# Half tiles of weights, whole float32 attention products, and a planner that counts issue time

## The chip, the core and the metric

The kernel runs on one core of a Trainium2 chip. The metric is device time in microseconds of one execution, the median of three. The engines of a core are TensorE (PE in the profile; its weight loads are PEld), VectorE (DVE), ScalarE (ACT), GpSimd (POOL) and SyncE (SP); each runs its own instruction stream in order, and DMA transfers are issued from SP, ACT and POOL. SBUF is the on-chip memory, PSUM the eight accumulator banks that TensorE writes.

## What is computed

One attention layer of a decoder and a final norm; `DEPTH` is 1, so the convolution layer does not run. There are 256 rows, a model width of 4096 and 32 heads of 128, all in float32.

```python
def attn_branch(xn, w_in, w_out):
    q, k, v, g = jnp.split(xn @ w_in, 4, axis=-1)     # 256x4096 @ 4096x16384
    o = stick_breaking_attention(heads(q), heads(k), heads(v))
    return (o * jax.nn.silu(g)) @ w_out               # 256x4096 @ 4096x4096

# per head, with z = q k^T / sqrt(128), for s < t:
log_fail = where(causal, log_sigmoid(-z), 0)
suffix   = cumsum(log_fail, reverse=True) - log_fail
a        = where(causal, exp(log_sigmoid(z) + suffix), 0)
out      = a @ v
# whole program
h   = x + attn_branch(rms_norm(x, norm_attn), w_in, w_out)
out = rms_norm(h, final_norm)
```

## The kernel before

**Split products.** A float32 operand is written as the sum of two float32r tiles, a high part (a cast on ACT) and a low part (full minus high, on DVE). One product is three TensorE passes: high by high, high by low, low by high (`mm3`, lines 752 to 758). The 335 MB of weights are split this way as they arrive: `piece` (lines 394 to 404) casts `raw` to `wh` on ACT and writes `wl` on DVE.

**Units and steps.** The projection by `w_in` is 16 units; unit u makes q and k, then gate and v, of two heads. The projection by `w_out` is a plain unit (number 16), two mixed units (17 and 18) and two single ones (19 and 20). A unit has 16 steps along the contraction, 256 rows of weights each. A mixed unit runs Strassen-like products: a step of the list `SEVEN` has seven products, the others eight, collected in seven PSUM banks `b1` to `b7`, which `combine` (lines 654 to 696) adds up on DVE and ACT into `qk_sb` and `gv_sb` (in the out projection, into the `h` tiles). A product is three matmuls of 128 by 128 by 512 columns, named `acc<-wh,nh`, `acc<-wl,nh` and `acc<-wh,nl` (`sh`, `oh`, `ph` and `rh` stand in place of `nh` in other units).

**Weights.** A step's weights are one quad: a `raw` tile of 8 KB in each partition, four slots of 512 columns, filled by four DMAs of 256 KB from SP (`load`, lines 341 to 360). A slot of 512 is two blocks of 256 columns, so the destination runs are 1 KB. There are three quads (`RAW_BUFS`), and a quad is given back when the low parts of all its pieces are written (`low_done`). For a seven step, `sums` (lines 375 to 392) adds slots in place, in three DVE instructions: one of 1024 columns and two of 512.

**Attention of a head** (`head`, lines 767 to 858): four transposes into `tr`; `tr` is split into `qkh` (ACT) and `qkl` (DVE); six matmuls give the scores `z`; ACT and DVE turn them into `f`, which is split into `fh` and `fl`; four matmuls scan; ACT makes `a`, which is split into `ah` (ACT) and `al` (DVE); v had been split once a unit into `vh` and `vl` (`v_parts`); six matmuls give `o`; DVE multiplies it by the gate.

**What sets the order.** All of it is decided ahead, while the program is built. `Plan` (lines 87 to 212) simulates the engines with fixed costs (`vector_ns`, `scalar_ns`, `tensor_ns`, and the issue costs in `moved`, line 320: 55 ns a DMA on SP, 900 on POOL). Each piece of work is a generator that waits for names (`until`), for rings of buffers (`take`, `give`) or for an engine (`work`). When an engine is free in the simulation, the waiting request with the smallest key, its due time, is written into that engine's stream. The chip then follows this order and waits wherever an input is late. Work for TensorE in `head` goes through `ten` (line 317), with a key ahead of all weight products, so it is put in as soon as the simulation has its inputs.

Every instruction is recorded through one helper, so the profile shows almost all of them under one line, L106; they are told apart by the names of their tiles.

Of the kernel before, what the change touches and what calls it, by code (L numbers as in the profile page):

```python
# [43 lines left out]
RAW_BUFS = 3  # L44
# [19 lines left out]
EIGHT_PARTS = (  # L64
    (slice(0, 2), ((2, "A11", 0), (2, "A12", 1), (4, "A21", 0), (4, "A22", 1))),
    (slice(2, 4), ((5, "A21", 0), (5, "A22", 1), (3, "S3", 0), (3, "S5", 1))),
# [3 lines left out]
def plain_part(place, one, two):  # L70

    return place, ((one, "A11", 0), (two, "A21", 0), (one, "A12", 1), (two, "A22", 1))
# [14 lines left out]
class Plan:  # L87
# [97 lines left out]
    def work(self, engine, cost, emit, key=None, after=None, hold=True, moves=()):  # L185

        def request(go):
            self.serial += 1  # L190
            item = (self.here if key is None else key, self.serial, cost, emit, after, go, hold, moves)
            heapq.heappush(self.waiting[engine], item)
            self.later(max(self.now, self.free[engine]), self.turn, engine)

        return request

    def turn(self, engine):
# [4 lines left out]
        end = self.now + cost  # L202
# [13 lines left out]
def kernel(  # L216
# [41 lines left out]
    for u, (kind, w, cols) in enumerate(units):  # L258
        for s in range(NS):
            if kind == "single":  # L260
# [3 lines left out]
                which = [plain_part(slice(2 * (s % 2), 2 * (s % 2) + 2), *b)]  # L264
            else:
                quads.append(tuple((w, c, s) for c in cols))
                if kind == "plain":
                    which = [
                        plain_part(slice(0, 2), PLAIN["C11"], PLAIN["C21"]),
                        plain_part(slice(2, 4), PLAIN["C12"], PLAIN["C22"]),  # L270
# [3 lines left out]
            for i, (place, prods) in enumerate(which):  # L274
                parts.append(
                    dict(u=u, s=s, i=i, last=i == len(which) - 1, place=place, prods=prods, quad=len(quads) - 1,
                         seven=which is SEVEN_PARTS, size=len(range(*place.indices(2 * KT))))
                )
# [30 lines left out]
    def dve(emit, n, key=None, **kw):  # L309
        cost = sum(vector_ns(m) for m in n) if isinstance(n, tuple) else vector_ns(n)  # L310
        return nc.work("vector", cost, emit, soon() if key is None else key, **kw)

    def act(emit, n, key=None, **kw):
        cost = sum(scalar_ns(m) for m in n) if isinstance(n, tuple) else scalar_ns(n)
# [15 lines left out]
    for name, places in (  # L330
        ("raw", RAW_BUFS), ("w", PAIRS), ("s", SINGLES), ("gh", 3), ("one", 1), ("two", 1), ("vh", 1), ("vl", 1),
        ("qkh", 1), ("qkl", 1), ("f", 1), ("ah", 1), ("al", 1), ("att", 1), ("heads", 1),
        *((f"b{b}", 1) for b in range(1, 8)),
    ):
        nc.ring(name, places)
# [3 lines left out]
    lows_left = {}  # L339

    def load():
        for q, given in enumerate(quads):
            yield nc.take("raw")
            raw[q] = wp.tile([P, 2 * KT, W], F32, tag="raw", name=f"raw{q}", bufs=RAW_BUFS)
            todo = []
            for k, (w, blocks, s) in enumerate(given):
                for chunks in ([slice(0, 1), slice(1, 2)] if q == 0 else [slice(0, 2)]):
                    to = slice(KT * k + chunks.start, KT * k + chunks.stop)
                    todo.append([
                        (raw[q][:, to, i * CW : (i + 1) * CW], w[c, s][:, chunks, :]) for i, c in enumerate(blocks)  # L350
                    ])
            for k, some in enumerate(todo):
                name = ("raw", q, k) if q == 0 else ("raw", q) if k else None
                yield moved(
                    "sync",
                    lambda some=some: [nc.sync.dma_start(*a) for a in some],
                    [W * (1 if q == 0 else KT) // 2] * 2,
                    quad_key[q],
                    after=name and (lambda name=name: nc.tell(name)),
                )  # L360

    quad_key, quad_parts = {}, {}
    for n, p in enumerate(parts):
        quad_key.setdefault(p["quad"], first[n])
        quad_parts.setdefault(p["quad"], []).append(n)

    def low_done(n):
        q = parts[n]["quad"]
        lows_left[n] -= 1
        if not lows_left[n]:  # L370
            nc.tell(("lows", n))
            if all(lows_left.get(m) == 0 for m in quad_parts[q]):
                nc.give("raw")

    def sums(q):

        a, b, c, d = quad_parts[q]
        r = raw[q]
        tt = nc.vector.tensor_tensor
        key = first[c] - 3.0 * 1e3  # L380
        yield nc.until(("lows", a), ("lows", b))
        yield dve(
            lambda: tt(
                out=r[:, 0:3:2, :], in0=r[:, 0:4:3, :], in1=r[:, 2:3, :].broadcast_to([P, 2, W]), op=ALU.add
            ),
            2 * W, key,
        )
        nc.tell(("sums", c))
        key = first[d] - 3.0 * 1e3
        yield dve(lambda: tt(out=r[:, 3, :], in0=r[:, 0, :], in1=r[:, 3, :], op=ALU.add), W, key)  # L390
        yield dve(lambda: tt(out=r[:, 1, :], in0=r[:, 3, :], in1=r[:, 1, :], op=ALU.add), W, key)
# [822 lines left out]
```

## Time and profile before

| | |
|---|---|
| median of 3 runs | 1800.3 us (1799.93 to 1800.44) |
| the profiled execution | 1805.19 us, span 1803.4 us |
| PE busy | 1768.4 us, 98% |
| DVE busy | 1611.2 us, 89% |
| ACT busy | 1145.4 us, 64% |
| weight DMAs on the SP queue | 1284, nearly all 256 KB, 4.6 to 4.8 us from issue to landing |
| bytes moved | 388 MB, 215 GB/s over the span |

The span is what the trace covers. The execution's own time is 1.8 us longer than its span, and 4.9 us over the median of the runs that were only timed. The end of a matmul is modelled in the trace, so a PE that starts a 512-column matmul every 0.23 us shows no idle time, though each is drawn 0.39 us long; the starts of matmuls tell its pace.

### The profile page before, as it was taken

To read this page: it belongs to the slowest core of one execution; us is meant where nothing else is said; L and a number is where in the kernel's file an instruction comes from. 1 tells how busy PE (TensorE), PEld (TensorE's weight loads), DVE (VectorE), ACT (ScalarE), POOL (GpSimd) and SP (SyncE) were. 2 spreads that over 40 slices of the span, in tenths; PEclk is the share of its full clock that TensorE was granted. 3 is DMA by queue.
4 is the path that set the end of the run, shared out by engine and by line. 5 is a ranking of instruction groups with operands and counts; after the bars stand their busy time and mean duration, and the time that the engine had idled before them with its cause. 6 is when DMAs were issued, how large, how long until landed. Compare 5 with 4: busy or idle time off the path is not lost.

```text
span 1803.4 us, 23678 instructions
## 1 busy us (share of the span) xinstructions
PE 1768.4 (98%) x8011; PEld 1450.0 (80%) x8011; DVE 1611.2 (89%) x1974; ACT 1145.4 (64%) x1568; POOL 67.0 (4%) x132
## 2 busy tenths in 40 slices
PE   9999999999999999999999999999999999999997
PEld 7888888878887888788888878887888778878786
DVE  6679999999999999999999999999999887999864
ACT  6675757576757675757575757675756565655543
POOL 0001000000000000000000000000002100000000
PEclk9999999999999999999999999999999999999999
DMA  9958575666666656575756565666669967678884
GB/s 319 318 179 269 153 221 181 211 195 206 182 212 193 214 181 212 180 233 171 231 175 223 177 214 190 202 197 194 202 189 279 310 190 226 215 226 254 252 270 159
DMA packets 373625, 388.01 MB, mean 215 GB/s; under 512 B 23808, under 2 KB 351744, under 8 KB 373504
## 3 DMA queue, kind: packets, MB, share of 16 engines
q1 hardware_dynamic: 357296, 352.15, 62.4%
q0 software_dynamic: 14624, 31.99, 5.6%
q10 hardware_dynamic: 1584, 2.38, 0.4%
q8 instruction: 62, 1.02, 0.2%
q14 instruction: 59, 0.48, 0.1%
HBM read 370.43 MB, written 15.99 MB: 214 GB/s over the span
## 4 chain that ended last, share of the span: by engine, by line
PE 63%; DVE 13%; DMA 10%; ACT 6%; issue 4%; SPq 3%; ACTq 0%; DVEq 0%
PE acc L106 59%; DMA raw<-in_w_in_dram 6%; DVE wl L106 6%; ACT wh L106 5%; DVE raw L106 4%; SPq L106 3%; DMA raw<-in_w_out_dram 3%; PE z L106 2%; PE o L106 1%; DVE gv_sb L106 1%; PE tr L106 1%; ACT f L106 0%; ACT qk_sb L106 0%; ACT h L106 0%; ACTq L106 0%
## 5 line engine op out<-in xcount | busy, mean ns | idle before, releaser
L106 ACT CAST wh<-raw 128x1024 fp32r<-128x1024 f32 (+1 forms) x898 | 857.5, 986 | 478.5 <-DVE raw L106 221.4
L106 DVE TENSOR_TENSOR wl<-raw,wh 128x1024 fp32r<-128x1024 f32 (+1 forms) x898 | 1003.1, 1142 | 138.5 <-ACT wh L106 124.0
L106 PE MATMUL acc<-wh,nh 128*128 128x512 f32 x1680 | 662.9, 395 | 0.0
L106 PE MATMUL acc<-wl,nh 128*128 128x512 f32 x1680 | 656.2, 391 | 1.0 <-DVE wl L106 0.6
L106 PE MATMUL acc<-wh,nl 128*128 128x512 f32 x1680 | 655.2, 390 | 0.0
L106 PEld LDWEIGHTS acc<-wl,nh 128*128 128x128 f32 x1680 | 315.9, 188 | 68.2 <-DVE wl L106 7.5
L106 PEld LDWEIGHTS acc<-wh,nl 128*128 128x128 f32 x1680 | 315.4, 188 | 66.5
L106 PEld LDWEIGHTS acc<-wh,nh 128*128 128x128 f32 x1680 | 315.7, 188 | 61.2
L106 DVE TENSOR_TENSOR raw<-raw 128x512 f32<-128x512 f32 (+1 forms) x384 | 332.6, 866 | 6.8
L106 PE MATMUL acc<-wl,ph 128*128 128x512 f32 x304 | 119.2, 392 | 3.5 <-DVE wl L106 3.3
L106 PE MATMUL acc<-wh,ph 128*128 128x512 f32 x304 | 118.8, 391 | 0.8 <-DVE h L106 0.8
L106 PE MATMUL acc<-wh,pl 128*128 128x512 f32 x304 | 118.4, 389 | 0.0
L106 PE MATMUL acc<-wh,sh 128*128 128x512 f32 x256 | 101.8, 398 | 0.6 <-DVE sh L106 0.6
L106 PE MATMUL acc<-wh,sl 128*128 128x512 f32 x256 | 101.1, 395 | 0.8 <-DVE sl L106 0.8
L106 PE MATMUL acc<-wl,sh 128*128 128x512 f32 x256 | 100.8, 394 | 0.0
L106 PEld LDWEIGHTS acc<-wl,ph 128*128 128x128 f32 x304 | 57.1, 188 | 17.9 <-DVE wl L106 6.3
L106 PEld LDWEIGHTS acc<-wh,ph 128*128 128x128 f32 x304 | 57.1, 188 | 14.6 <-DVE h L106 1.5
L106 PEld LDWEIGHTS acc<-wh,pl 128*128 128x128 f32 x304 | 57.1, 188 | 11.6
L106 PEld LDWEIGHTS acc<-wh,sl 128*128 128x128 f32 x256 | 48.7, 190 | 11.7 <-DVE sl L106 1.5
L106 PEld LDWEIGHTS acc<-wh,sh 128*128 128x128 f32 x256 | 48.9, 191 | 11.3 <-issue 1.5
L106 PEld LDWEIGHTS acc<-wl,sh 128*128 128x128 f32 x256 | 48.9, 191 | 9.9
L106 ACT CAST qkh<-tr 128x512 fp32r<-128x512 f32 x32 | 18.8, 588 | 56.6 <-PE tr L106 56.5
(130 smaller groups left out, 1393.8 us busy)
## 6 DMA issues: line engine op xcount, KB each, us to landing
raw<-in_w_in_dram SPq DMA_DIRECT2D x1020, 256.0 KB, 4.6
raw<-in_w_out_dram SPq DMA_DIRECT2D x256, 256.0 KB, 4.8
xr<-in_x_dram SPq DMA_DIRECT2D x16, 256.0 KB, 5.7
xn<-in_xT_dram POOLq DMA_DIRECT2D x16, 256.0 KB, 4.0
xres<-in_x_dram SPq DMA_DIRECT2D x16, 256.0 KB, 5.3
xs<-in_xT_dram SPq DMA_DIRECT2D x15, 256.0 KB, 5.7
spill_f<-gated POOLq DMA_DIRECT2D x15, 256.0 KB, 3.6
spill_h<-oh POOLq DMA_DIRECT2D x15, 256.0 KB, 5.1
```

What stands on the lines that cost most here:

```text
L106: return self.tc.keep_in_program_order(getattr(self.engine, name)(*args, **kw))
```

## The change

- **Half tiles.** A quad becomes two `raw` tiles of 4 KB in each partition, one for each pair of column blocks, laid out block by block, so that a DMA of 256 KB writes runs of 2 KB. There are seven such tiles in place of three quads. Each is given back by itself (`tile_done`). `sums` makes four DVE instructions of 512 columns in place of three. The third and fourth part of a seven step are grouped anew (banks 7 and 6, then 5 and 4).
- **Whole products.** The scores and attention times v take float32 operands, with one matmul where there were three: `tr` is only copied (`qkT`, ACT), `a` and v are used as they are. `v_parts`, `qkl`, `ah` and `al` are gone. The scan keeps its split.
- **The planner's numbers.** A DMA on SP or ACT costs 330 ns. An ACT instruction that starts after idle time costs 50 ns more; grouped instructions are costed one by one with 122 or 100 ns between them. A request by `ten` is only entered 400 ns after its inputs are there.
- **Room.** Two `h` tiles of column block 5 move to the ring `s`; the early `xs` tiles use `qkh` and `qkl` in place of `vh` and `vl`, and the constant `neg_tri` is made earlier, to free `qkl`.

```diff
-RAW_BUFS = 3
+RAW_BUFS = 7
+BOTH, SECOND = slice(0, 2), slice(1, 2)
 SEVEN_PARTS = (
-    (slice(0, 2), ((1, "A11", 0), (2, "A12", 1))),
-    (slice(3, 4), ((3, "S4", 0),)),
-    (slice(0, 3, 2), ((5, "S1", 0), (7, "S3", 1))),
-    (slice(1, 4, 2), ((4, "A22", 0), (6, "S2", 1))),
+    (0, BOTH, ((1, "A11", 0), (2, "A12", 1))),
+    (1, SECOND, ((3, "S4", 0),)),
+    (1, BOTH, ((7, "S3", 0), (6, "S2", 1))),
+    (0, BOTH, ((5, "S1", 0), (4, "A22", 1))),
 )
...
+            if wait:
+                self.later(self.now + wait, ready, go)
...
-        end = self.now + cost
+        end = self.now + cost + (50 if engine == "scalar" and self.now > self.free[engine] else 0)
...
+    FULL_P, FULL_S = (P,) * 4, (S,) * 4
     def ten(emit, *n):
-        return nc.work("tensor", sum(tensor_ns(m) for m in n), emit, nc.here - 1e4)
+        return nc.work("tensor", sum(tensor_ns(m) for m in n), emit, nc.here - 1e4, wait=400)
     def moved(engine, emit, sizes, key, after=None, hold=False, adds=False):
-        issue = {"sync": 55, "gpsimd": 900, "scalar": 90}[engine]
+        issue = 900 if engine == "gpsimd" else 330
...
+            for t, (w, blocks, s) in enumerate(given):
+                yield nc.take("raw")
+                r = raw[q, t] = wp.tile([P, HG, KT, CW], F32, tag="raw", name=f"raw{q}_{t}", bufs=RAW_BUFS)
...
+                    def both():
+                        for i, c in enumerate(blocks):
+                            nc.sync.dma_start(r[:, i, chunks, :], w[c, s][:, chunks, :])
...
+    def tile_done(*tile):
+        tile_left[tile] -= 1
+        if not tile_left[tile]:
+            nc.give("raw")
...
+        yield nc.until(("lows", a), ("raw", q, 1))
+        yield add(one, 0, one[:, :, 0, :], two[:, :, 0, :], first[c])
+        yield add(two, 0, two[:, :, 0, :], two[:, :, 1, :], first[c])
+        yield nc.until(("lows", b))
+        yield add(two, 1, two[:, :, 1, :], one[:, :, 0, :], first[c])
+        nc.tell(("sums", c))
+        yield add(one, 1, one[:, :, 1, :], two[:, :, 1, :], first[d])
...
-        yield act(lambda: nc.scalar.copy(qh, tr), 2 * S)
-        yield dve(lambda: minus(ql, tr, qh), 2 * S)
+        qk = ap.tile([P, 2, S], F32, tag="qkh", name=f"qkT{u}_{i}")
+        yield act(lambda: nc.scalar.copy(qk, tr), 2 * S)
...
-            mm3(z[:, 0:P], k(slice(P, S)), q(slice(P, S)), True, False)
-            mm3(z[:, P:BW], k(slice(0, P)), q(slice(0, S)), False, True)
+            nc.tensor.matmul(z[:, 0:P], qk[:, 1, P:S], qk[:, 0, P:S], start=True, **kw)
+            nc.tensor.matmul(z[:, P:BW], qk[:, 1, 0:P], qk[:, 0, :], start=False, **kw)
...
-        yield act(lambda: nc.scalar.copy(ah, a), BW)
-        yield dve(lambda: minus(al, a, ah), BW)
...
-            mm3(o, v(0), (ah[:, P:BW], al[:, P:BW]), True, False)
-            mm3(o[:, P:S], v(1), (ah[:, 0:P], al[:, 0:P]), False, True)
+            nc.tensor.matmul(o, v(0), a[:, P:BW], start=True, stop=False, **kw)
+            nc.tensor.matmul(o[:, P:S], v(1), a[:, 0:P], start=False, stop=True, **kw)
```

The order moves in two places that the prediction speaks of. The first is on TensorE, at the change from unit 8 to unit 9 (`acc8_3` is the last bank of unit 8; `tr8_0` the transposes of its first head; `z8_0` its scores). Before:

```order
L106 MATMUL acc8_3_6748<-wh399_7397,nh15_1987 128x512
L106 MATMUL acc8_3_6748<-wl399_7398,nh15_1987 128x512
L106 MATMUL acc8_3_6748<-wh399_7397,nl15_1988 128x512
L106 MATMUL tr8_0_7483<-ident_118,qk_sb8_7409 128x128 x4
L106 MATMUL acc8_3_6748<-wh399_7397,nh15_1987 128x512
L106 MATMUL acc8_3_6748<-wl399_7398,nh15_1987 128x512
L106 MATMUL acc8_3_6748<-wh399_7397,nl15_1988 128x512
L106 MATMUL acc9_2_7496<-wh400_7416,nh0_1047 128x512
```

With the change:

```order
L108 MATMUL acc8_3_6702<-wl399_7344,nh15_1961 128x512
L108 MATMUL acc8_3_6702<-wh399_7343,nl15_1962 128x512
L108 MATMUL acc9_2_7438<-wh400_7359,nh0_1067 128x512
L108 MATMUL acc9_2_7438<-wl400_7360,nh0_1067 128x512
L108 MATMUL acc9_2_7438<-wh400_7359,nl0_1068 128x512
L108 MATMUL tr8_0_7437<-ident_100,qk_sb8_7353 128x128 x4
L108 MATMUL acc9_2_7438<-wh400_7359,nh0_1067 128x512
L108 MATMUL acc9_2_7438<-wl400_7360,nh0_1067 128x512
```

The transposes stand six matmuls later: 16 in place of 10 after the last one into bank 4, whose sum they read. In both orders the scores follow soon, nine matmuls after the transposes before and six with the change; the third step of both heads' chains, the scan, stands 48 and 30 matmuls after the scores in both.

The second place is the SP queue in unit 18, where steps of the out projection load weights (`raw296` and on) between rows of x (`xres`). Before:

```order
L106 DMA xres3_0_14977<-in_x_dram 128x512
L106 DMA raw296_14986<-in_w_out_dram 128x2x256 x4
L106 DMA raw297_15001<-in_w_out_dram 128x2x256 x4
L106 DMA xres3_1_15068<-in_x_dram 128x512
L106 DMA raw298_15076<-in_w_out_dram 128x2x256 x4
L106 DMA raw299_15093<-in_w_out_dram 128x2x256 x4
```

With the change:

```order
L108 DMA xres3_0_14894<-in_x_dram 128x512
L108 DMA raw297_0_14897<-in_w_out_dram 128x512 x2
L108 DMA raw297_1_14911<-in_w_out_dram 128x512 x2
L108 DMA raw298_0_14918<-in_w_out_dram 128x512 x2
L108 DMA raw298_1_14977<-in_w_out_dram 128x512 x2
L108 DMA xres3_1_14985<-in_x_dram 128x512
L108 DMA raw299_0_14992<-in_w_out_dram 128x512 x2
```

Each quad's four DMAs become two pairs, each pair behind a wait of its own, and the weights stand one quad further ahead of the rows of x.

More of the change, by code (lines that the diff above doesn't have):

```diff
@@ L338 @@
     raw, wh, wl = {}, {}, {}
-    lows_left = {}
+    lows_left, tile_left = {}, {}
+    quad_parts = {}
+    for n, p in enumerate(parts):
+        quad_parts.setdefault(p["quad"], []).append(n)
+        tile_left[p["tile"]] = tile_left.get(p["tile"], 0) + 1
     def load():
         for q, given in enumerate(quads):
[L343 to L360, printed above, removed]
@@ L535, in blocks_all @@
             nc.start(blocks_of(i))
+    nc.start(nc.take("qkl") for _ in range(1))
     together(blocks_of(0), load(), blocks_all())
@@ L883, in heads @@
     def heads(u):
-        together(v_parts(u), gate(u))
+        nc.start(gate(u))
         yield nc.until(("qk", u))
```

147 lines of the change are left out of this document (70 added, 77 removed).

## The prediction

> **What bounds the kernel now.** I read the page first, then the busy time by windows, then who waited for whom, then single instructions in order of time. The page's parts 1 and 4:
>
> ```profile
> PE 1768.4 (98%) x8011; PEld 1450.0 (80%) x8011; DVE 1611.2 (89%) x1974; ACT 1145.4 (64%) x1568; POOL 67.0 (4%) x132
> PE 63%; DVE 13%; DMA 10%; ACT 6%; issue 4%; SPq 3%; ACTq 0%; DVEq 0%
> ```
>
> TensorE sets the time, but a 98% made of modelled ends hides short stalls, so its starts must be counted. Two windows of 100 us in the out projection, where no attention is mixed in (the first columns are PE and the number of its matmuls, then PEld, DVE, ACT, POOL, the clock and the DMA share):
>
> ```profile
> 1500.00:1600.00 100.00, 100.00 (x443) 82.84 (x442) 88.03 (x114) 58.15 (x80) 2.15 (x4) 1.00 0.71 217
> 1600.00:1700.00 100.00, 95.66 (x409) 75.60 (x408) 92.72 (x100) 56.74 (x69) 7.83 (x15) 1.00 0.76 239
> ```
>
> Undisturbed, a matmul starts every 100/443 = 0.226 us. The second window starts 34 fewer, 34 x 0.226 = 7.7 us lost. All else that TensorE loses inside the span is of three kinds. The waits, and the group of the weight products for its drawn length:
>
> ```profile
> PE tr L106 <- DVE qk_sb L106: 11.0, 12, 1.5
> PEld z L106 <- DVE qkl L106: 8.6, 23, 1.5
> L106 PE MATMUL acc<-wh,nh 128*128 128x512 f32 x1680 | 662.9, 395 | 0.0
> ```
>
> About once a unit the transposes of the first head wait for the bank sums. Each of the 12 stalls hides another 0.395 - 0.226 = 0.17 us behind the drawn end of the matmul before it: 11.0 + 12 x 0.17 = 13.0 us. The scores wait a little for the low part of q and k. The third is the change to the out projection, in windows of 10 us:
>
> ```profile
> 1420.00:1430.00 10.00, 9.39 (x41) 7.17 (x41) 9.90 (x11) 6.76 (x8) 2.44 (x5) 1.00 0.81 246
> 1430.00:1440.00 10.00, 8.90 (x44) 7.19 (x43) 7.74 (x10) 3.10 (x4) 1.29 (x3) 1.00 1.03 333
> 1440.00:1450.00 10.00, 8.33 (x37) 6.57 (x36) 6.90 (x9) 9.21 (x15) 0.00 (x0) 1.00 0.68 212
> 1450.00:1460.00 10.00, 9.11 (x29) 7.23 (x29) 7.74 (x16) 5.43 (x11) 0.54 (x1) 0.66 0.67 200
> ```
>
> PE is busy 35.7 of 40 us, and after the idle the granted clock falls to 0.66 for 10 us: 4.3 + 3.4 = 7.7 us. So some 31 us of stalls lie on TensorE's path, 13.0 + 2 to 3 + 7.7 + 7.7.
>
> **What lies behind the late losses.** The chain of waits, in the second window (start, us, what):
>
> ```profile
> 1681.17 0.61 SPq L106
> ...
> 1681.83 5.39 DMA raw<-in_w_out_dram
> ...
> 1687.32 0.63 ACT wh L106
> ```
>
> A quad given back frees SP, which issues four DMAs, 0.61 us each; the last one's landing, 5.4 us later, frees ACT, then DVE's low part, then the next quad. That loop, not the bytes, is late: the DMA share there is 0.76.
>
> **Part 1, half tiles.** Bytes and number of DMAs are the same. What one issue costs by its destination runs, from the views of the tiles `raw` (1 KB runs) and `xr` (2 KB runs, as `raw` will have):
>
> ```profile
> L106 SPq DMA_DIRECT2D raw<-in_w_in_dram x1028: 327/610/1554, 0.8 to 1414.4; - x172
> L106 SPq DMA_DIRECT2D xr<-in_x_dram x16: 328/334/557, 15.6 to 64.7; - x16
> ```
>
> Four issues fall from 4 x 0.61 = 2.4 to 4 x 0.33 = 1.3 us, and the first half can be used two DMAs earlier. Seven halves are 3.5 quads against 3; a seven step is 21 matmuls, 4.75 us, so the ring covers half a step, 2.4 us, more. Together about 3.5 us a turn, against waits that this row lists:
>
> ```profile
> ACT wh L106 <- DMA raw<-in_w_out_dram: 33.0, 21, 3.5
> ```
>
> The longest is 3.5 us, the mean 1.6. So most of them go. But DVE is busy 92.7 of 100 us there and is the next to be late, so of the 7.7 us I take back 5. At the change to the out projection the DMA share reaches 1.03, with the reloads of spilled heads beside the weights; a deeper ring helps and the bytes don't shrink: 4 of 7.7 us. If neither comes back, these are 0; at most both come back, 15. At the start, the fourth `xs` load stands behind the fifth quad on SP: 0 to 2 us lost; I take 0, since TensorE needs it only in the fourth step.
>
> DVE's sums change from three instructions to four, by these rows and those of what Part 2 removes:
>
> ```profile
> L106 DVE TENSOR_TENSOR raw<-raw 128x512 f32<-128x512 f32 x256 | 176.3, 689 | 4.7
> L106 DVE TENSOR_TENSOR raw<-raw 128x1024 f32<-128x1024 f32 x128 | 156.3, 1221 | 2.1
> L106 DVE TENSOR_TENSOR qkl<-tr,qkh 128x512 fp32r<-128x512 f32 x32 | 21.9, 683 | 1.6 <-ACT qkh L106 1.6
> L106 DVE TENSOR_TENSOR al<-a,ah 128x384 fp32r<-128x384 f32 x32 | 17.7, 552 | 0.1
> L106 DVE TENSOR_TENSOR vl<-gv_sb,vh 128x512 fp32r<-128x512 f32 x16 | 11.0, 685 | 2.5 <-ACT vh L106 2.5
> L106 ACT CAST ah<-a 128x384 fp32r<-128x384 f32 x32 | 16.4, 512 | 0.7 <-DVE a L106 0.7
> L106 ACT CAST vh<-gv_sb 128x512 fp32r<-128x512 f32 x16 | 9.9, 616 | 12.6 <-DVE gv_sb L106 12.6
> ```
>
> 512 x 0.689 - 332.6 = +20.2 us in all, 0.16 a seven step. It hides under TensorE, except where DVE itself is late.
>
> **Part 2, whole products.** DVE loses 21.9 + 17.7 + 11.0 = 50.6 us, net of the sums 30.4 of 1611.2; ACT loses 26.3 of 1145.4. TensorE covers both, so they count for nothing by themselves; they make room before the stalls. The wait of `z` for `qkl` loses its cause: 3 us back (2 to 8). On the path lies what TensorE pays. Scores of one head now, from the timeline (start, length):
>
> ```profile
> 903.98 0.33 PE L106 MATMUL z<-qkh 128*128 128x128 f32 x1 [0.15 <-DVE qkl L106]
> 904.14 0.27 PE L106 MATMUL z<-qkl,qkh 128*128 128x128 f32 x1
> 904.26 0.27 PE L106 MATMUL z<-qkh,qkl 128*128 128x128 f32 x1
> 904.37 0.33 PE L106 MATMUL z<-qkh 128*128 128x256 f32 x1
> 904.54 0.28 PE L106 MATMUL z<-qkl,qkh 128*128 128x256 f32 x1
> 904.65 0.28 PE L106 MATMUL z<-qkh,qkl 128*128 128x256 f32 x1
> 904.77 0.40 PE L106 MATMUL acc<-wh,nh 128*128 128x512 f32 x1
> ```
>
> Six passes take 904.77 - 903.98 = 0.79 us, and a pass with weights of its own about 0.11 at 128 columns and 0.12 at 256. The six of `o`, first and last:
>
> ```profile
> 939.56 0.28 PE L106 MATMUL o<-ah,vh 128*128 128x256 f32 x1
> ...
> 940.20 0.44 PE L106 MATMUL acc<-wh,nh 128*128 128x512 f32 x1
> ```
>
> 0.64 us. No row shows a whole float32 product. It has to form the fourth partial product, low by low, that the split leaves out. With four passes at the pace above, a pair costs 4 x 0.11 + 4 x 0.12 = 0.92 us. Below, four passes at the streaming pace, 0.226 x 128/512 = 0.057 and 0.113 us: 0.68. Above, if each of the eight weight loads stood open, by this row:
>
> ```profile
> L106 PEld LDWEIGHTS acc<-wh,nh 128*128 128x128 f32 x1680 | 315.7, 188 | 61.2
> ```
>
> 8 x 0.188 + 0.68 = 2.18 us. I take 0.92, as every neighbouring pass loads its own weights and none shows its load in full. A head then pays 2 x 0.92 - 0.79 - 0.64 = +0.41 us, 32 heads +13.1 us; by the lower end -2.2, by the upper +93.
>
> The Trainium skill, FP8 and Floating Point Precision, section TensorE Precision Notes, says that true FP32 takes four passes through the array, H by H, H by L, L by H and L by L. It speaks against the change, three passes becoming four; by it the sum lies between -2.2 and +13.1, depending on how the loads are hidden, and a cheaper product would be ruled out. No row of this trace shows it.
>
> **Part 3, the planner.** The transposes stand six matmuls later behind bank 4, 1.4 us, and bank 6 is full six matmuls earlier. The stalls there are 1.1 us on average with their hidden part, 1.5 at most as drawn. So 11 of 13 us come back; none, if DVE comes later by as much. The scores now follow six matmuls behind the transposes, 1.36 us, in which ACT must copy `tr`, 0.59 us by this row; without the low part on DVE that fits:
>
> ```profile
> L106 ACT CAST qkh<-tr 128x512 fp32r<-128x512 f32 x32 | 18.8, 588 | 56.6 <-PE tr L106 56.5
> ```
>
> **The sum.** -11 - 3 - 4 - 5 + 13.1 = -9.9 us, so the profiled span goes from 1803.4 to 1793.5. The median shown lies 3.1 us under that span; I take the difference over: 1800.3 - 9.9 = 1790.4, about 1790.
>
> **The rivals.** (1) The whole product is cheap: its loads hide and it runs at 0.68 us or less a pair. For: no row says that a pass of a whole product must wait for its load; against: the 128-column passes of `z` do, 0.11 us against 0.057 by streaming. -23 - 2.2: 1775. (2) Slower: the stalls only move. The wait of `tr` turns up in the next thing that DVE owes (`f`, the low parts behind the new order), for DVE is as full as it was but for 2%, and the late loop turns at DVE's pace. Then only the 3 us of `z` come back, against 13.1 paid: 1800.3 + 10 = 1810. It decides as soon as less than 13.1 us of the 23 are recovered. For: 92.7% on DVE in the window with the stalls. Against: ACT waits there for DMA landings, which come earlier. (3) The weight loads of a whole product stand open, up to 2.18 us a pair: +93 - 23, 1870. The change loses from 0.72 + 23/64 = 1.07 us a pair on. (4) Gain and price cancel, the half tiles and the new costs having no effect that shows: 13 us recovered, 1800.
>
> **Chances.** The forecast 0.45, (1) 0.20, (2) 0.20, (3) 0.05, (4) 0.10. About 0.2%, 3.6 us, is what a measurement of this kernel can tell from no change. Faster by more: 0.45 + 0.20 = 0.65; within: 0.10; slower: 0.25. The likeliest case alone spans 1780 to 1797, by recovering 18 to 28 us and a price of 8 to 13. The range takes in most of (1) and of (2): 1771 to 1809.
>
> **What would show it.** The starts around `z<-qkT` and `o<-a`: 0.92 us a pair, or 0.68, or over 1.07. The row of `tr` waiting for `qk_sb`: under 3 us. The 100 us of the out projection with the fewest matmuls: 430 or more. Four windows of 10 us at the change of projections: PE over 37.5. SP's issue of `raw`: 334 ns. DVE near 1581 us. I am wrong if the pair costs over 1.07 us, or if PE idles as before at `tr` or in the out projection.

## The result

The changed kernel takes 1774.1 us (median of 4 runs, 1771.4 to 1775.1) against 1800.1 us for the kernel before (1796.8 to 1800.4): a ratio of 0.9857, 95% interval 0.984 to 0.9874, so 26 us faster where 10 were forecast. The profiled executions stand further apart, by 31.2 us of span (1803.4 to 1772.2), since that of before lay 5 us above its median; what follows from the traces is an account of these two executions. The page of the changed kernel, parts 1, 4 and 6:

```profile
PE 1752.9 (99%) x7883; PEld 1444.6 (82%) x7883; DVE 1584.7 (89%) x2022; ACT 1117.2 (63%) x1520; POOL 66.9 (4%) x132
PE 91%; DVE 4%; ACT 2%; DMA 2%; issue 1%; SPq 0%; ACTq 0%; DVEq 0%
raw<-in_w_in_dram SPq DMA_DIRECT2D x1020, 256.0 KB, 4.0
```

TensorE now carries 91% of the chain that ended last, where it had 63%; VectorE and the DMAs fell from 13% and 10% to 4% and 2%. VectorE's busy time fell by 26.5 us and ScalarE's by 28.2, about the sizes that the instructions give. The two windows of the out projection, and the four of the change of projections:

```profile
1500.00:1600.00 100.00, 98.14 (x427) 79.36 (x425) 93.55 (x117) 58.36 (x75) 0.00 (x0) 1.00 0.61 202
1600.00:1700.00 100.00, 99.39 (x438) 82.04 (x438) 88.42 (x101) 54.44 (x67) 8.48 (x16) 1.00 0.86 279
...
1420.00:1430.00 10.00, 10.00 (x48) 8.36 (x47) 8.97 (x13) 8.50 (x15) 0.54 (x1) 1.00 0.80 252
1430.00:1440.00 10.00, 10.00 (x50) 8.29 (x48) 7.92 (x15) 6.02 (x11) 0.54 (x1) 1.00 0.75 240
1440.00:1450.00 10.00, 10.00 (x48) 8.41 (x47) 8.60 (x16) 6.95 (x12) 1.07 (x2) 1.00 0.52 173
1450.00:1460.00 10.00, 10.00 (x47) 8.10 (x46) 8.24 (x16) 6.87 (x13) 0.54 (x1) 1.00 0.67 227
```

The weaker of the two windows of 100 us had 409 matmuls before and has 427 now. At the change of projections PE has no idle time left and the granted clock stays at 1.00. TensorE's waits, then ScalarE's for the weights of the out projection (us in total, times, longest):

```profile
PE acc L108 <- DVE wl L108: 2.1, 4, 0.8
PE acc L108 <- DVE sl L108: 2.0, 1, 2.0
PE warm L108 <- DVE idle L108: 1.3, 1, 1.3
PE acc L108 <- DVE sh L108: 0.8, 1, 0.8
PE o L108 <- ACT gated L108: 0.7, 2, 0.4
```

```profile
ACT wh L108 <- DMA raw<-in_w_out_dram: 4.2, 3, 3.2
```

The 11.0 us of `tr` are gone from the list, and of ScalarE's 33.0 us for landings 4.2 are left. What was disputed, a pair of whole products, in the timeline (start, length; x4 is four records drawn as one row), for `z` and for `o`:

```profile
892.74 0.82 PE L108 MATMUL z<-qkT 128*128 128x128 f32 x4
893.20 0.58 PE L108 MATMUL acc<-wh,nh 128*128 128x512 f32 x1
893.62 0.40 PE L108 MATMUL acc<-wl,nh 128*128 128x512 f32 x1
...
908.74 0.81 PE L108 MATMUL o<-a,gv_sb 128*128 128x256 f32 x4
909.31 0.47 PE L108 MATMUL acc<-wh,nh 128*128 128x512 f32 x1
909.62 0.39 PE L108 MATMUL acc<-wl,nh 128*128 128x512 f32 x1
```

A pair is two products, so each is two records. The first weight product behind is held up too: from the pair's start to the second weight product pass 0.88 us, less one pitch of 0.226 that is 0.65 us, for both. Six split passes cost, counted in the same way over all 32 heads, 0.76 us for `z` and 0.69 for `o` in the median; the whole pairs 0.66 and 0.67.

Where the 31.2 us of span came from, by the starts of TensorE's matmuls (a group's cost runs from its first start until weight products go on at their pitch; what weight products start late is added up by place):

| us | before | after | difference |
|---|---|---|---|
| transposes `tr` | 27.8 | 14.1 | -13.7 |
| scores `z` | 24.1 | 21.1 | -3.0 |
| scan | 21.2 | 18.4 | -2.8 |
| `o`, transposes and products | 30.3 | 29.0 | -1.3 |
| weight products, first 40 us | 4.1 | 6.2 | +2.2 |
| weight products, 40 to 1400 us | 10.9 | 8.1 | -2.8 |
| weight products, change of projections | 6.4 | 0.4 | -6.0 |
| weight products, out projection | 8.0 | 4.7 | -3.3 |

With 0.4 us less at the warm-up this is the difference of the spans to within 0.1 us. The rows of weight products also hold the time by which a head's step starts late after a weight product, a wait for its own input: before `z` 3.2 us before (1.3 of them at the change of projections) and 0.2 after, before the scan 1.8 and 0, before the products of `o` 0 and 1.3.

### The profile page after: what moved, and what is told of

Read it like the earlier page. It is cut to its first block, busy times and chain, and to the rows that moved or that the text cites. A ratio compares the mean times of both kernels' runs of the same rounds, so it can differ in the third digit from the quotient of the medians.

```text
span 1772.2 us, 23794 instructions
## 1 busy us (share of the span) xinstructions
PE 1752.9 (99%) x7883; PEld 1444.6 (82%) x7883; DVE 1584.7 (89%) x2022; ACT 1117.2 (63%) x1520; POOL 66.9 (4%) x132
## 4 chain that ended last, share of the span: by engine, by line
PE 91%; DVE 4%; ACT 2%; DMA 2%; issue 1%; SPq 0%; ACTq 0%; DVEq 0%
PE acc L108 87%; PE z L108 2%; DVE wl L108 2%; PE o L108 2%; DMA xres<-in_x_dram 1%; DVE raw L108 1%; PE tr L108 1%; ACT wh L108 1%; DMA raw<-in_w_in_dram 1%; DVE h L108 1%; ACT h L108 0%; SPq L108 0%; ACTq L108 0%; ACT f L108 0%; DVE nl L108 0%
## 5 line engine op out<-in xcount | busy, mean ns | idle before, releaser
L108 ACT CAST wh<-raw 128x1024 fp32r<-128x1024 f32 (+1 forms) x898 | 845.1, 986 | 422.8 <-DVE raw L108 204.9
L108 DVE TENSOR_TENSOR wl<-raw,wh 128x1024 fp32r<-128x1024 f32 (+1 forms) x898 | 990.5, 1141 | 125.6 <-ACT wh L108 119.3
L108 DVE TENSOR_TENSOR raw<-raw,raw 128x512 f32<-128x512 f32 x384 | 264.7, 689 | 8.8
L108 DVE TENSOR_TENSOR raw<-raw 128x512 f32<-128x512 f32 x128 | 88.3, 690 | 3.4
L108 PEld LDWEIGHTS acc<-wh,ph 128*128 128x128 f32 x304 | 57.1, 188 | 13.1 <-ACT wh L108 0.6
```

Of the source, the lines that this page charges most:

```text
L108: return self.tc.keep_in_program_order(getattr(self.engine, name)(*args, **kw))
```

## Experiments

All ratios are to the kernel before on the same chip, with 95% intervals; that kernel itself ran between 1791 and 1807 us there, so the intervals decide. Theories on trial at first: **C**, a whole product runs at the streaming pace and the parts' gains add up; **D**, the relief of VectorE and ScalarE does it by itself. Later come **E** (the whole products pay by VectorE's relief) against **F** (they pay on TensorE), and **G**, **H** and **I** (the seventh tile, the lag and the issue cost each count).

### One part at a time

Whole products alone, in the kernel before (planner's numbers and quads as they were):

```diff
-        yield act(lambda: nc.scalar.copy(qh, tr), 2 * S)
-        yield dve(lambda: minus(ql, tr, qh), 2 * S)
+        yield act(lambda: nc.scalar.copy(qk, tr), 2 * S)
...
-            mm3(o, v(0), (ah[:, P:BW], al[:, P:BW]), True, False)
+            nc.tensor.matmul(o, v(0), a[:, P:BW], start=True, stop=False, **kw)
```

> The kernel before, with the whole float32 products for scores and attention times v and nothing else of the change. Theory C (a whole product runs at the streaming pace, so it costs nothing, and the gain comes from the order and the weight tiles): scores plus products with v cost 0.1 us a head less than before, 3 to 4 us in all; the transposes wait for the bank sums about as before (over 6 us), so 1800 falls to about 1793 to 1797. Theory D (the gain comes from the vector and scalar work taken away): the transposes' waits vanish and the change of projections runs through, 1780 or less. The forecast on record had +13 us of price here: 1805 or more.

Half tiles alone; beside the split's tiles only six fit, not seven. The numbers are the old ones, except that an issue counts 330 ns in the first 120 us of the plan (this holds for all runs with half tiles and the old issue cost):

```diff
-RAW_BUFS = 3
+RAW_BUFS = 6
+                r = raw[q, t] = wp.tile([P, HG, KT, CW], F32, tag="raw", name=f"raw{q}_{t}", bufs=RAW_BUFS)
```

> The change with split products put back and the planner's old numbers, with six half tiles for want of room: half tiles, 2 KB runs and the new grouping of the seven step alone (the first 120 us of the plan keep the new issue cost). Theory C: the stalls at the change of projections and in the out projection go (8 and 3 us) and the transposes' waits fall, as bank 6 is full six matmuls earlier: 1780 to 1787. Theory D: vector work is 20 us more than before, so no gain: 1798 to 1805.

The planner's numbers alone:

```diff
+        return nc.work("tensor", sum(tensor_ns(m) for m in n), emit, nc.here - 1e4, wait=400)
+        issue = 900 if engine == "gpsimd" else 330
```

> The kernel before, with the planner's new numbers alone: the first transposes of a unit stand 13 instead of 10 or 13 matmuls behind bank 4, the scores 18 instead of 9 or 15 behind them. Theory C: part of the 13 us at the transposes comes back, the out projection stays: 1788 to 1795. Theory D: 1797 to 1803, as the work on the engines is the same.

Half tiles (six) and the numbers, with the split products:

```diff
-RAW_BUFS = 7
+RAW_BUFS = 6
+            mm3(z[:, 0:P], k(slice(P, S)), q(slice(P, S)), True, False)
```

> The change with the split products put back (the low parts of q and k, of the weights a and of v on the vector engine again), with six half tiles for want of room. Theory C: the whole products are worth 3 to 4 us: 1777 to 1782. Theory D: the vector engine is late again, the transposes wait over 6 us: 1790 or more.

Measured: whole products 1.0015 (0.9999 to 1.0032), half tiles 1.0041 (1.0027 to 1.0056), the numbers 0.9993 (0.9979 to 1.0008), the last two together 0.9953 (0.9934 to 0.9971). No part alone gains anything. C's sum falls. D falls on the whole products alone, where it had 1780 or less and 1800.6 were measured; its times for the other three (1803.8, 1795.9 and 1790.5 us measured) are about right, but in the last of them the waits at `tr` that it named do not show (0.2 us); those for `wl` do (14.0). TensorE's waits for whole products alone, then for the numbers alone:

```profile
PE z L106 <- DVE fl L106: 5.1, 10, 0.8
PE z L106 <- ACT qkT L106: 3.8, 6, 1.8
PE tr L106 <- DVE qk_sb L106: 2.6, 3, 1.2
PE o L106 <- ACT gated L106: 2.2, 5, 0.9
```

```profile
PE acc L106 <- DVE wl L106: 11.0, 15, 1.9
PE z L106 <- DVE fl L106: 3.2, 5, 1.1
PE z L106 <- DVE qkl L106: 3.2, 1, 3.2
PE tr L106 <- DVE qk_sb L106: 2.0, 3, 1.4
```

Each takes most of the 11.0 us away from `tr`, and gets them back elsewhere: with whole products at the scan (`fl`), the scores (`qkT`) and `o`, with the numbers at the low parts of the weights, and with the half tiles alone there too (12.7 us, with no row for `qk_sb`). That is the prediction's second rival, the stalls only move, in each part by itself.

### Taking one thing back from the change

VectorE's work back: 80 subtractions that nothing reads, of the sizes of the dropped low parts and at their places in the plan. They add 36.6 us to VectorE's busy time, less than the 50.6 that the change dropped, and the plan's order moves with them a little (30 matmuls between scores and scan become 33):

```diff
+            yield dve(lambda: minus(spare[:, 0:n], spare[:, 0:n].bitcast(F32), spare[:, 0:n]), n)
...
+        nc.start(dead(2 * S))
```

> The change, with vector work of the same shapes and number as the low parts that it dropped (32 of 512 and 32 of 384 columns for the heads, 16 of 512 for v, 50 us) put back at the same places, into a tile that nothing reads; TensorE's work and order stay. Theory E (the whole products pay because they take vector work away): the weight products wait for their low parts again, as with the split products, 1784 to 1792. Theory F (they pay on TensorE, by fewer passes and shorter chains): 1773 to 1778.

Six half tiles in place of seven:

```diff
-RAW_BUFS = 7
+RAW_BUFS = 6
```

> The change with six half tiles in place of seven, the control for the split products put back, which had six. Theory E: the seventh tile is worth little, 1773 to 1779, and most of the 16 us between that kernel and the change belongs to the whole products. Theory G (the seventh tile is what was missing there): 1786 or more.

The lag taken out of the plan:

```diff
-emit, nc.here - 1e4, wait=400)
+emit, nc.here - 1e4)
```

> The change without the 400 ns that a request for TensorE waits in the plan: the transposes stand 13 instead of 16 matmuls behind bank 4. Theory H (the lag keeps TensorE from waiting for inputs that the chip has later than the plan): waits of 0.3 to 1 us a unit at the transposes and at the scans come back, 1780 to 1792. Theory E alone: 1773 to 1778.

The old issue cost again, after the first 120 us of the plan:

```diff
-        issue = 900 if engine == "gpsimd" else 330
+        issue = 900 if engine == "gpsimd" else 330 if nc.now < 1.2e5 else {"sync": 55, "scalar": 90}[engine]
```

> The change with the planner's old issue cost of 55 ns a DMA on SP after the first 120 us of the plan. Theory I (counting the issue time matters, as the plan otherwise hands tiles to scalar and vector before they land): the scalar engine waits for landings again, 1778 to 1790. Against it: with 2 KB runs an issue takes 0.33 us and four half tiles of slack lie between, so 1773 to 1777.

Measured: dead work 0.9924 (0.9907 to 0.9941), six halves 0.9937 (0.9915 to 0.9959), no lag 0.9956 (0.9941 to 0.9972), 55 ns 0.9927 (0.9909 to 0.9945). By the ratios each loses 12 to 18 us of the 26 (8 to 17 by the medians); the four losses add up to 57, more than twice the gain, so they are not shares of it. G, H and I hold in direction, and E too; with 55 ns ScalarE waits 115.9 us for weights of `w_in` to land, where the change has 53.2. With the dead work VectorE is busy 1621.3 us, a little over the 1611.2 of before, and TensorE's weight loads wait for the low parts of weights 34 times instead of 19 (dead work, then the change):

```profile
PEld acc L108 <- DVE wl L108: 19.2, 34, 1.6
```

```profile
PEld acc L108 <- DVE wl L108: 8.4, 19, 1.1
```

So 37 us of room on VectorE are worth 9 to 12 us here, though TensorE sets the time: F alone does not explain the change. Without the lag the waits lie in the heads:

```profile
PEld o L108 <- ACT gated L108: 12.7, 28, 0.8
PEld tr L108 <- DVE qk_sb L108: 6.5, 9, 1.2
PEld z L108 <- ACT qkT L108: 5.2, 13, 0.4
PEld z L108 <- DVE fl L108: 5.1, 17, 0.6
```

### The price, the pieces, the old numbers, a truer cost

Scores issued twice. The second pair's sums replace the first's:

```diff
+            nc.tensor.matmul(z[:, 0:P], qk[:, 1, P:S], qk[:, 0, P:S], start=True, **kw)
+            nc.tensor.matmul(z[:, P:BW], qk[:, 1, 0:P], qk[:, 0, :], start=False, **kw)
```

> The changed kernel with the pair of whole score products issued twice for each of the 32 heads (the first pair's sums are overwritten by the second; the plan counts both). 32 more pairs on TensorE, nothing more on VectorE or ScalarE. The price of a whole pair on the path is then the added time over 32. Theory C (whole products run at the streaming pace, two records of each at half rate): 0.66 us a pair, +21 us against the changed kernel, so about 1796 us and a ratio of 0.998. The prediction's own price: 0.92 us a pair, +29 us, 1804 us, ratio 1.002. Theory K (the longer TensorE time gives VectorE more air, so part of the price is hidden): +14 us or less, 1788 us or less, ratio under 0.994.

Pieces of 1 KB, by another layout of the half tiles:

```diff
-                r = raw[q, t] = wp.tile([P, HG, KT, CW], F32, tag="raw", name=f"raw{q}_{t}", bufs=RAW_BUFS)
+                r = raw[q, t] = wp.tile([P, KT, HG, CW], F32, tag="raw", name=f"raw{q}_{t}", bufs=RAW_BUFS)
```

> The changed kernel with each half tile of raw weights laid out so that its 256 KB come in pieces of 1 KB, not 2 KB; seven half tiles and all else as in the change (the two blocks of a pair lie apart in it, so the operand adds read 512 columns in two pieces). Theory J (the ring's depth is what pays, the size of the pieces is not): the weights' landing goes back from 4.0 to about 4.6 us, SP's issue of one from 0.33 to about 0.61 us, and the time stays within 2 us of the changed kernel, ratio 0.985 to 0.987. Theory M (the pieces pay by themselves, since the planner now counts 0.33 us an issue and SP would take 0.61): it loses as much as the run with 55 ns issue cost or more, +8 us or more, ratio 0.990 or above, with TensorE's waits for wl (VectorE's low parts of weights) above 6 us where the changed kernel has 2.1.

The change without `wait`, and with the old `dve`, `act` and issue costs:

```diff
-emit, nc.here - 1e4, wait=400)
+emit, nc.here - 1e4)
-        end = self.now + cost + (50 if engine == "scalar" and self.now > self.free[engine] else 0)
+        end = self.now + cost
```

> The changed kernel with all of the planner's old numbers after the first 120 us of its plan (no lag of 400 ns, no 122 and 100 ns between pieces, no 50 ns for ScalarE's start, SP's issue at 55 ns): whole products and seven half tiles alone. Theory L (the parts need each other: each removed stall comes back at another place unless the order fits): it is worse than either of the two runs that took back one number each (ratio 0.9956 without the lag, 0.9927 with 55 ns): 0.995 to 1.000, with waits both at tr (VectorE's qk_sb, 4 us or more) and at the weights (wl, 6 us or more). Theory C' (the layout and the products carry the gain and the planner's numbers add only their own single effects): 0.9857 plus nothing to 0.0099 for the lag, at most 0.9956.

A truer cost of a whole pair in the plan:

```diff
-    FULL_P, FULL_S = (P,) * 4, (S,) * 4
+    FULL_P, FULL_S = (P,) * 2, (2 * S - 32,) * 2
```

> The changed kernel, but the plan counts a whole pair at 0.645 us, near what the trace of the changed kernel shows (0.66 us); the change counts it at 0.92 us. If the order is as sensitive to such costs as the runs with one number taken back suggest, the time may move by some us either way. Theory N: a better fit of costs gives 2 to 6 us more, 1768 to 1772 us, ratio 0.982 to 0.984, with TensorE's starts at weight products losing less than the 8 us that they lose in the changed kernel between 40 and 1400 us. Its rival, that the order is already at what VectorE and TensorE allow: within 2 us, ratio 0.985 to 0.987; or a change of order that costs (0.988 or more).

**Scores twice**: 1.0028 (1.0016 to 1.004), 1803.9 us, 30 more than the change. At first sight that is the prediction's 0.92 us a pair. By the starts of matmuls, the scores themselves go from 21.1 to 42.0 us: 20.9 / 32 = 0.65 us a pair, C's price. K, which had part of it hidden, falls. The other 8 us are stalls of an order that is not the change's any more: 3.7 at the scan, 1.3 at `tr`, 3.0 at weight products between 40 and 1400 us. Total time alone would have misled.

**Pieces of 1 KB**: 0.9919 (0.9889 to 0.9948), 9 us lost by the medians, 11 by the ratios. The issue of one transfer, from the view of `raw` (shortest/median/longest, ns), with 1 KB and in the change:

```profile
L108 SPq DMA_DIRECT2D raw<-in_w_in_dram x1028: 328/556/2047, 0.8 to 1394.6; - x172
```

```profile
L108 SPq DMA_DIRECT2D raw<-in_w_in_dram x1028: 327/376/1499, 0.8 to 1389.1; - x172
```

The landing is 4.4 us instead of 4.0. VectorE's sums and low parts and ScalarE's casts last as long as in the change, so it is the transfers that got slower. J falls: the pieces pay, not the ring's depth alone. M's bounds hold; the waits for `wl` are 5.6 us, a little under its 6.

**Old numbers**: 1.0167 (1.0139 to 1.0195), 55 us over the change and slower than the kernel before. C' falls; L holds in direction, and its 0.995 to 1.000 was far too mild:

```profile
PE acc L108 <- DVE wl L108: 13.5, 22, 0.8
PE tr L108 <- DVE qk_sb L108: 10.4, 12, 0.9
PE z L108 <- DVE fl L108: 7.5, 16, 0.5
PE o L108 <- ACT gated L108: 4.9, 8, 1.6
```

**A truer cost** in the plan: 0.9952 (0.9936 to 0.9969), 16 us worse than the change. N falls. The waits for `wl` are 16.3 us. A plan that believes the measured price makes a worse order than one that believes 0.92, though the chip's work is the same; why was not settled.

### Is the order a lucky one?

The losses so far could also mean that any shift of the order costs (theory Q) rather than that the parts need each other (L). The numbers were moved by a hair, and the combination that was missing was run. An issue counted at 340 ns:

```diff
-        issue = 900 if engine == "gpsimd" else 330
+        issue = 900 if engine == "gpsimd" else 340
```

> The changed kernel, but the plan counts 340 ns for each weight transfer's issue instead of 330 ns: nothing that the chip does is other, only the order of some instructions (the order of matmuls differs first after 1,127 of them). Theory L (the parts need each other, and a hair's shift of a number changes nothing of that): within 3 us of the changed kernel, ratio 0.984 to 0.9875. Theory Q (the order is a pick: any shift of it moves the time by as much as the runs that took a part back): up to 18 us more, ratio 0.989 to 0.996, and with it most of the waits for wl that those runs showed (7 us or more at TensorE's matmuls).

ScalarE's start at 55 ns:

```diff
-        end = self.now + cost + (50 if engine == "scalar" and self.now > self.free[engine] else 0)
+        end = self.now + cost + (55 if engine == "scalar" and self.now > self.free[engine] else 0)
```

> The changed kernel, but the plan adds 55 ns instead of 50 ns where ScalarE starts after an idle time. The order differs first after 138 matmuls. Theory L: within 3 us of the changed kernel, ratio 0.984 to 0.9875. Theory Q: ratio 0.989 to 0.996, waits for wl of 7 us or more.

The kernel before with an issue counted at 65 ns:

```diff
-        issue = {"sync": 55, "gpsimd": 900, "scalar": 90}[engine]
+        issue = {"sync": 65, "gpsimd": 900, "scalar": 90}[engine]
```

> The kernel before, but the plan counts 65 ns for each weight transfer's issue instead of 55 ns: its order differs from early on, its work does not. Theory L: within 3 us of the kernel before, ratio 0.998 to 1.002. Theory Q: the time moves by 5 us or more either way, ratio outside 0.997 to 1.003.

The kernel before with whole products and all the new numbers:

```diff
-            mm3(z[:, 0:P], k(slice(P, S)), q(slice(P, S)), True, False)
+            nc.tensor.matmul(z[:, 0:P], qk[:, 1, P:S], qk[:, 0, P:S], start=True, **kw)
...
+        return nc.work("tensor", sum(tensor_ns(m) for m in n), emit, nc.here - 1e4, wait=400)
```

> The kernel before with whole score and value products and with all of the planner's new numbers, but three raw tiles in pieces of 1 KB as before: the combination of two parts that is missing. Theory L (needs all three): 0.993 to 1.000. Theory R (VectorE's relief and the numbers are what it takes, the ring's depth adds what the run with six half tiles lost, 8 us or more): 0.990 to 0.994, with the wait at tr for qk_sb gone (under 1 us) and the waits for wl at 7 us or more. Theory Q: anywhere from 0.990 to 1.010.

Measured: 340 ns 0.9872 (0.9849 to 0.9895; 1773.5 us), 55 ns for ScalarE 0.9879 (0.9857 to 0.99; 1775.0 us), within 1 us of the change by their medians and 3 to 4 us over it by the ratios; the second lies just above L's 0.9875. TensorE's waits for `wl` are 3.9 and 3.2 us, well under Q's 7. The kernel before with 65 ns: 1.0027 (1.0009 to 1.0044), a little more than L allowed and less than Q asked. So Q falls for shifts as small as these, and they are small: both leave the steps of the heads where the change has them. For larger shifts it is not excluded. The truer cost changes nothing but the order either, and costs 16 us.

Whole products with the numbers: 0.9903 (0.9876 to 0.993), 1778.9 us. Two parts that gain nothing alone take away 17 us by the ratio and 19 by the medians together. L, which needed all three (0.993 or more), falls: two are enough for two thirds of the gain. Theory R's bounds hold it, but its waits for `wl` of 7 us or more do not show: they are 1.4 us.

### Which of the numbers, and a better start

```diff
+        return nc.work("tensor", sum(tensor_ns(m) for m in n), emit, nc.here - 1e4, wait=400)
```

in the kernel before with whole products, the other numbers old:

> The kernel before with whole score and value products, and of the planner's new numbers only the lag of 400 ns; three raw tiles in pieces of 1 KB. Theory S (whole products need the lag, since the plan otherwise sets the scan six products behind the scores; the other numbers are small): 0.988 to 0.994, TensorE's waits for fl (14.3 us at the weight loads and 5.1 at the matmuls in the run of whole products alone) under 3 us in all. Theory T (the costs of the pieces and of an issue are what makes the order fit): 0.997 or above, with waits for wl of 10 us or more at the matmuls.

The better start:

```diff
-                yield nc.take("raw")
+                if q or not t:
+                    yield nc.take(*["raw"] * (1 if q else len(given)))
```

> The changed kernel, but the plan takes both raw tiles of the first four blocks at once, so that all eight of their transfers are issued ahead of the second piece of activations, as in the kernel before (in the change that piece goes out between them). The rest of the order is the change's from the second unit on. Theory U (the first 40 us lose 6.2 us in the change against 2.1 in the run without half tiles by this): 2 to 4 us less, 1770 to 1772 us, ratio 0.983 to 0.985. Its rival: the tail of the scatter, within 1 us, 0.9855 to 0.988.

The lag alone with whole products: 0.9947 (0.9927 to 0.9968), between the bounds of S and T. From 1.0015 it takes 0.7 percentage points, where all the numbers together take 1.1. Waits for `fl` fall from 14.3 to 5.4 us at the weight loads, where S had under 3; what is left stands at `o`:

```profile
PE o L106 <- ACT gated L106: 11.3, 14, 1.9
```

The other numbers take this to 0.6 us. The better start: 0.9876 (0.9857 to 0.9896), 1774.9 us, no gain. The first 40 us lose 4.3 instead of 6.2 us, and the units behind 9.8 instead of 8.1. The stall at 6 us, before the first matmul that reads `sl` (the low part of the activations), hardly moves, from 2.4 to 2.2 us; what differs is the granted clock behind it, 0.82 between 10 and 15 us with 19 matmuls, where the change has 0.53 and 14. U falls, and no run here beat the change.

### What the runs say together

| ratio to before | old numbers | new numbers |
|---|---|---|
| split products, quads | 1 | 0.9993 |
| split products, six halves | 1.0041 | 0.9953 |
| whole products, quads | 1.0015 | 0.9903 |
| whole products, seven halves | 1.0167 | 0.9857 |

The column of old numbers never gains; the new numbers are worth nothing in the first row and 3% in the last. Why the whole products need them can be read from TensorE's order. Counted in weight matmuls (0.226 us each) that stand between two steps of a head in units 2 and up, commonest values first:

| | scores to scan | scan to `o` |
|---|---|---|
| before | 48, 30, 24 | 27, 21, 24 |
| whole products, old numbers | 48, 27 | 12, 9 |
| whole products, seven halves, old numbers | 21, 45 | 9, 12 |
| whole products, lag alone | 30, 51 | 12, 21 |
| whole products, all numbers | 51, 36 | 18, 15 |
| the change | 30, 48 | 12, 15 |

The plan puts a step in as soon as its simulation has the inputs. Splitting `a` was an ACT and a DVE step (0.51 and 0.55 us) between the scan and `o`. Take them out, and the plan draws `o` up from 21 or more matmuls to 9 or 12, which are 2.0 to 2.7 us. It had counted ACT and DVE too fast all along: 525 ns for a copy of 512 columns that takes 588, 600 for a subtraction that takes 683. The long way had covered that; with the way short, TensorE stands there. The waits for `fl` at the weight loads with whole products, half tiles and old numbers, with whole products alone, and with the lag added to these:

```profile
PEld z L108 <- DVE fl L108: 18.9, 30, 0.9
PEld z L106 <- DVE fl L106: 14.3, 29, 1.1
PEld z L106 <- DVE fl L106: 5.4, 17, 0.5
```

The short distances are 21, 27 and 30 there, and at the change's 30, with all numbers, the row is not in the list. The lag puts 3 to 9 matmuls back. The distance is not all: without the lag, but with the other new numbers, the wait is 5.1 us at 27. This is read from the orders and the waits; no run moved a scan or an `o` by itself. It does not explain the other loss, the waits for `wl` with six halves, 1 KB pieces, the dead work and the truer cost: there the distances in the heads are about the change's (33 and 12 for the truer cost), and it is the ring, the transfers or VectorE that come late.

## Why the prediction was wrong

**The step that failed: the price in Part 2.** "I take 0.92, as every neighbouring pass loads its own weights" put +13.1 us on the path. Measured on the path are 0.65 to 0.67 us a pair, under the lower end of 0.68, so the products of the scores and of `o` fall: by 3.0 and 0.9 us, -3.9 in all. These 17 us are four fifths of the 21.3 us by which the span was missed (-9.9 forecast, -31.2 measured), and about all of the 16 us by which the medians were (26 against 10). The 3 us for `qkl` came back as forecast: they are what `z` started late, 3.2 us before and 0.2 after, and stand in the table's rows of weight products. The neighbouring passes were the wrong row: with a load for each pass they go at about 0.11 us with 128 columns and 0.12 with 256, and a whole product has only two loads. Its rows in the tile view show two for each of the 64 products:

```profile
L108 PEld LDWEIGHTS z<-qkT x128: 187/190/193, 102.3 to 1441.1; 128*128 128x128 f32 x128
L108 PE MATMUL z<-qkT x128: 270/327/383, 102.5 to 1441.4; 128*128 128x128 f32 x64, 128*128 128x256 f32 x64
```

The rule of the Trainium skill (FP8 and Floating Point Precision, section TensorE Precision Notes), four passes for true FP32, agrees with the trace: four times 0.057 and 0.113 us is 0.68 against 0.65. What the prediction drew from it, that four passes in place of three speak against the change, was wrong, since the split's three passes ran at their loads' pace and not at the streaming pace. The first rival, a cheap product and 1775 us, is what happened. Its hit within 1 us is partly luck: it had 25 us less, and the two traced executions differ by 31. The measured 1774.1 us lies outside the 1780 to 1797 of the likeliest case, and inside the range only because that took in this rival.

**"They count for nothing by themselves"** (Part 2, on VectorE and ScalarE) fell as well: 37 us of dead work on VectorE cost 9 to 12 us (with an order moved a little). Here a share of 89% on an engine off the path still decides how late each low part of a weight is.

**The recoveries had the right sizes and a wrong reason.** `tr` came back by 13.7 us (11 taken), the change of projections by 6.0, or 4.7 without the wait of `z` (4), the out projection by 3.3 (5). But Part 3 gave `tr` to the planner and Part 1 gave the late loop to the half tiles, each by itself. By itself each moved its stall to another place. For the out projection the half tiles are not even needed: weight products start 4.7 us late there with whole products alone and 2.9 with the numbers alone, both with quads, against 8.0 before and 4.7 with the change; and the run with 340 ns, with all seven half tiles, has 7.8, so 3.3 us lie within what such runs differ by. Beside these terms, the scan's 2.8 us and about 2 us at weight products in the units were not in the sum. The start, taken as 0, lost 2.2 us, just over its bound of 2, and half of it at 6 us, not in the fourth step (a stall of 2.4 us before the first matmul that reads `sl`, 1.4 before).

**What was to show it.** The weaker 100 us of the out projection were to hold 430 matmuls (427), PE to be over 37.5 us in the four windows (40.0), SP's issue 334 ns (376), DVE near 1581 us (1584.7), `tr` under 3 us (not listed): nearly all as said. Only the pair was not.

**The second rival**, the stalls only move, 1810 us: true of each part alone, and the whole products with half tiles and the old numbers came to 1829. The forecast's argument against it, ACT's earlier landings, is worth 5 to 8 us (half tiles added to whole products and the numbers) or 9 to 11 (pieces of 1 KB), by medians and ratios; what keeps the stalls of the heads from coming back is the lag and the other numbers.

## What to carry to other kernels

Where a plan made ahead sets the order, a cheaper step shortens the plan's distances too, and a cost model that was too fast then shows as new waits; measure such a change together with the plan's margins, not part by part. Cost an operation that the trace lacks by counting its loads and its streamed columns apart: a neighbour's pace may be that of its load. And when an experiment lengthens a path, read its price from the starts around it, since the total also has the order's reply.

## What was not expected of the hardware

A whole float32 product is two weight loads (about 190 ns each, as long as those of the weight products) and two records, not four. The 384 columns of a pair, twice, take 0.65 us; at the pace of a float32r weight product 2 x 384 x 0.226 / 512 = 0.34 us, so each record goes at about half that pace. So with the 128 and 256 columns here it is no dearer than three float32r passes with a load each: 0.66 against 0.76 us for `z`, 0.67 against 0.69 for `o`. And a 256 KB transfer's issue on SP depends on the length of its pieces: 556 to 610 ns in the median with 1 KB, 376 with 2 KB; 556 is the changed kernel with only the layout of its tiles turned, 610 the kernel before.
